# A decoder layer on one core: attention probabilities turned by VectorE blocks and SBUF transfers, value products in 128 rows, scores in eleven visits

## The chip, the core and the metric

One of the cores of one Trainium2 chip runs the whole layer. The metric is the device time of one execution in microseconds (us). A kernel's time is the median of its runs.

## The reference, cut to what matters

The layer takes x (512 positions x 1024) and mixes it in two ways. Mixer A is sparse attention with 8 heads of 64 in two groups of 4. Each query attends in three branches: to 31 compressed blocks, to selected blocks of 64 keys, and to a window of 512 keys. With 512 positions there are 8 blocks and up to 16 are selected, so the selected branch sees every earlier key, as the window does. The two therefore differ by their keys and values alone. Mixer B is a gated linear recurrence (HGRN2) with 4 heads.

```python
h = x @ w_in[l] + b_in[l]            # 5912 columns
ss = einsum('bghqd,bgqld->bghql', qr, ksel) * scale
ps = masked_softmax(ss, msel)        # the same for the window: sw, pw
o_slc = einsum('bghql,bgqld->bghqd', ps, vsel)
out_a = gt0 * o_cmp + gt1 * o_slc + gt2 * o_win
y = sigmoid(gm_a) * ((out_a * silu(z_a)) @ w_branch_a) + sigmoid(gm_b) * (o_b @ w_branch_b)
x = layer_norm(alpha * x + y @ w_out, ln_g, ln_b)
```

All is float32.

## The kernel before, in words

A float32 product is made of three products of a rounded kind: each operand is split by `split2` into a rounded part (a ScalarE cast) and a rest (a VectorE subtraction), and hi x hi, hi x lo, lo x hi are summed in PSUM.

**Projections.** The input projection runs in tiles of 128 output columns by 512 positions, named in `M_TILES`: qb, the keys and values, q, the gates z, and the merge gates ga and gb in pairs. `proj` computes one: 8 pieces of the contraction by three products, 24 products of 512 columns. At its start it issues the load of the weights three tiles ahead and the split of those two tiles ahead; three buffers hold each of raw, hi and lo. `SEQ` is the order of the tiles after qb and i. The tile v is computed as four groups of products of 280 columns (`proj_v`). Then come the two branch projections in the order of `BRANCH`, and the output projection with the layer norm.

**The weave.** TensorE and SP (whose queue issues nearly all DMAs) execute in the order in which the program is written; VectorE and ScalarE are ordered by a scheduler at build time. The order on TensorE is set by hand: `_Weave.tick` is called four times in a tile (twice in each of the four groups of v, twice for each half tile of the branches), and each tick resumes those chains (Python generators) that are due. A chain writes some instructions and yields a number of ticks; these numbers are in the table `D`. So attention, the recurrence and the compression are laid between quarter tiles of projections.

**Attention.** Positions are handled in blocks of 128 queries, i = 3 down to 0, over 128 * (i + 1) keys. Six units (i, branches): the two branches apart for i = 3 and 2, together for 1 and 0. `attn_scores` starts after q3 and needs both keys, all four q tiles and the gates. A visit computes scores of one m (a pair of heads, ab = 0 and 1, in the lower and upper 64 rows of the array at once; three products each), two of them in the first unit: 22 visits. `masked` adds the mask and takes the row's extreme on VectorE, then ScalarE makes the exponential and its sum. When a unit is complete its probabilities are scaled by gate over sum, half by ScalarE, half by VectorE.

`attn_values` turns the probabilities on TensorE: for each step of 128 keys, sixteen transposes of 64 queries x 128 keys against an identity, into two PSUM banks, which `split2` evicts in two halves of 512 columns. Then four products of 512 columns add up `accs`. There are 8 + 6 + 4 + 2 = 20 steps. The compressed branch's values are put into `asum` first; `finish` adds each block's result to it. At the end `asum` is gated by silu(z_a) and split for the branch projection.

**Rows.** From ga1 to gb2 (`ROWS`, `LAST`) the projections run in halves of 64 rows (`proj_rows`), two tiles side by side, so that score visits there do not change the array's row form; `row_half` does the same for value products, with hand-overs through an empty GpSimd instruction.

**Buffers.** t2 has 63 buffers of 512 columns, t4 has 4 of 1024. The compression weights w1s lie in eight t2 buffers.

Of the kernel before, what the change touches and what calls it, by code (L numbers as in the profile page):

```python
# [18 lines left out]
P = 128  # L19
# [5 lines left out]
ROWS, LAST = "ga1", "gb2"  # L25

# [14 lines left out]
SEQ = "kcmp vcmp kslc kwin q0 q1 v zb0 q2 zb1 q3 zb2 zb3 za0 za1 za2 za3".split()  # L41
# [30 lines left out]
D = dict(h0=8, h2=4, h3=6, h4=2, h5=8, h6=4, n0=3, n1=2, n2=9, c0=1, c1=6, c2=7, c3=7,  # L72
         r0=5, p0=4, p1=9, p2=1, b0=2, a0=3, a1=0, a3=1, a4=1, a5=1, s0=15, s2=0, s3=1, a6=1, v0=2, v1=3, v2=2, v3=3, w0=2, w1=1, w2=2, w3=4, a7=2, a8=1)


class _Weave:


    def __init__(self):
        self.now, self.runs, self.late, self.edge = 0, [], [], 0  # L80
# [16 lines left out]

# [6 lines left out]
def layer_kernel(ctx: ExitStack, tc: tile.TileContext, xT, xn, w0, wi, wf, wv, small, brow, consts,  # L104
# [18 lines left out]
    t2 = ctx.enter_context(tc.tile_pool(name="t2", bufs=63))  # L123
    t4 = ctx.enter_context(tc.tile_pool(name="t4", bufs=4))
# [9 lines left out]
    def T4():  # L134
        return t4.tile([P, 2, 512], F32R, name="t4", tag="t4")
# [145 lines left out]

    LOWER, UPPER, FULL = slice(0, 64), slice(64, 128), slice(0, 128)
    narrow, half = [False], {}

    ORDER = mybir.DependencyInfo(mybir.DependencyClass.Sync, mybir.DependencyReason.DATA)

    def hand_over(*last):
        step = tc.keep_in_program_order(G.nop()).ins
        for m in last:
            tc.add_manual_dep(step, m.ins.name, ORDER, reason="last product in the rows before")  # L290
        return step

    def take(step, m):
        tc.add_manual_dep(m.ins, step.name, ORDER, reason="one bank, other rows of the array")

    def proj_any(name):
        return (proj, proj_rows)[M_INDEX[ROWS] <= M_INDEX[name] <= M_INDEX[LAST]](name)

    def product(ps, i, kt, x, r, start, stop):
        w, b = parts[i][x == 2], (xh, xl)[x == 1]  # L300
        return T.matmul(ps, w[r, 128 * kt:128 * kt + 128], b[kt][r], start=start, stop=stop)

    def products3(ps, i, kt):
        for x in range(3):
            product(ps, i, kt, x, FULL, kt == 0 and x == 0, kt == KT - 1 and x == 2)

    def proj_rows(name):
        i = M_INDEX[name]
        load(i + 3)
        split(i + 2)  # L310
        if i not in half:
            half[i] = PA()
            for kt in range(4):
                if kt % 2 == 0:
                    weave.tick()
                products3(half[i], i, kt)
            narrow[0] = True
        ps = half.pop(i)
        weave.edge = weave.now
        if i == M_INDEX[LAST]:  # L320
            narrow[0] = False
            for kt in range(4, KT):
                if kt % 2 == 0:
                    weave.tick()
                products3(ps, i, kt)
            return ps, 4 + i
        weave.tick()
        nxt = half[i + 1] = PA()
        for q in range(8):
            if q == 4:  # L330
                step = hand_over(one, two)
            if q in (2, 4, 6):
                weave.tick()
            lo, up = (LOWER, UPPER) if q < 4 else (UPPER, LOWER)
            for x in range(3):
                one = product(ps, i, 4 + q % 4, x, lo, False, q == 7 and x == 2)
                two = product(nxt, i + 1, q % 4, x, up, q == 0 and x == 0, False)
                if q == 4 and x == 0:
                    take(step, one)
                    take(step, two)  # L340
        return ps, 4 + i
# [225 lines left out]
    def cmp_kv():  # L567
        yield D["c1"]
        while None in mvs:
            yield 1  # L570
        hp = PS()
# [11 lines left out]
        yield D["c2"]  # L583
        ps = PT()
# [5 lines left out]
        yield D["c3"]  # L590
        ps = PT()
# [52 lines left out]
    def cmp_scores():  # L644

        while "cmp" not in ready:
            yield 1
        pg = PS(), PS()
# [11 lines left out]
    def cmp_probs(g, src):  # L660
        ps = transpose4(src)
# [17 lines left out]
        yield D["p1"]  # L679
        ps = transpose4(s)  # L680
# [5 lines left out]
    probs, pv_at = {}, [0]  # L686


    slot, alone = [-1, 0], [False]

    def visit(i):
        if weave.now != slot[0]:
            if narrow[0]:
                if (weave.now - weave.edge) % D["w%d" % i]:
                    return False
            elif weave.now < slot[1]:
                return False
        slot[:] = weave.now, weave.now + D["v%d" % i]
        return True
# [511 lines left out]
```

## Time and profile before

| | |
|---|---|
| time, median of 3 runs | 428.81 us (428.34 to 428.9) |
| span of the profiled execution | 427.3 us |
| what lies around the span, by the median of the runs | 1.5 us |
| TensorE busy | 420.1 us, 98% |
| VectorE busy | 290.2 us, 68% |
| ScalarE busy | 240.7 us, 56% |
| DMA moved | 47.6 MB, mean 111 GB/s |

The span runs from the first to the last instruction of one profiled execution; the page gives no other time of that execution. PE is TensorE's products, PEld its weight loads, DVE is VectorE, ACT ScalarE, POOL GpSimd, SP the queue that issues DMAs. A product's duration is its latency: products overlap, and what one costs is the distance between starts.

### The profile page before, as it was taken

How to read it: one execution, taken by the hardware profiler on the slowest of the kernel's cores; microseconds unless marked ns; L12 is line 12 of the kernel's file. 1: busy time of each engine (PE TensorE's matmuls, PEld its weight loads, DVE VectorE, ACT ScalarE, POOL GpSimd, SP SyncE). 2: the span in 40 equal slices, each digit the busy share in tenths (PEclk: the TensorE clock that was granted, in tenths of full speed). 3: DMA queues.
4: the chain of work that ended last, by engine and by line, in shares of the span. 5: the costliest groups of instructions: out<-in, count | busy, mean ns of one | idle time of the engine just before them, and what ended most of it. 6: DMA issues, size and time to landing. Idle time of an engine off the chain costs nothing.

```text
span 427.3 us, 6625 instructions
## 1 busy us (share of the span) xinstructions
PE 420.1 (98%) x2471; PEld 347.2 (81%) x2471; DVE 290.2 (68%) x592; ACT 240.7 (56%) x489; POOL 9.9 (2%) x22
## 2 busy tenths in 40 slices
PE   8999999999999999999999999999999999999994
PEld 7888888888898878876878978777788888888884
DVE  4925578995665569867665677368466977873683
ACT  3534533624346535588676777678687865538301
POOL 2000000000001220000000000000000000000000
PEclk9999999999999999999999999999999999999998
DMA  8995600243340555311311131111433640153031
GB/s 266 377 392 146 218 0 2 74 125 81 108 135 2 138 188 166 98 52 49 100 51 51 51 98 51 50 51 49 149 122 102 222 129 20 51 164 132 3 147 49
DMA packets 21024, 47.60 MB, mean 111 GB/s; under 512 B 2944, under 2 KB 4864, under 8 KB 20992
## 3 DMA queue, kind: packets, MB, share of 16 engines
q1 hardware_dynamic: 20560, 46.79, 33.5%
q8 instruction: 19, 0.31, 0.3%
q10 hardware_dynamic: 432, 0.39, 0.3%
q14 instruction: 13, 0.11, 0.1%
HBM read 41.93 MB, written 2.10 MB: 103 GB/s over the span
## 4 chain that ended last, share of the span: by engine, by line
PE 97%; DMA 1%; DVE 0%; SPq 0%; issue 0%; DVEq 0%; ACT 0%; ACTq 0%
PE pa L112 62%; PE pss L112 16%; PE pso L112 11%; PE pst L112 4%; PE pst L116 3%; DMA t<-in_w_dram 1%; SPq L119 0%; DVE t L1128 0%; PE pss L116 0%; DVE t L203 0%; DVE t L1125 0%; DVEq L1207 0%; ACT t L1123 0%; DVE sm_ss L1126 0%; ACTq L1123 0%
## 5 line engine op out<-in xcount | busy, mean ns | idle before, releaser
L112 PE MATMUL pa<-t,whi 128*128 128x512 f32 (+1 forms) x688 | 201.7, 394 | 0.0
L112 PEld LDWEIGHTS pa<-t,whi 128*128 128x128 f32 (+1 forms) x688 | 120.5, 188 | 26.9 <-issue 3.1
L112 PE MATMUL pa<-t,wlo 128*128 128x512 f32 (+1 forms) x344 | 127.1, 391 | 0.0
L160 DVE TENSOR_TENSOR wlo<-wraw,whi 128x1024 fp32r<-128x1024 f32 x46 | 56.5, 1232 | 43.9 <-ACT whi L159 42.7
L159 ACT CAST whi<-wraw 128x1024 fp32r<-128x1024 f32 x46 | 48.3, 1049 | 48.6 <-PE pa L112 33.8
L112 PEld LDWEIGHTS pa<-t,wlo 128*128 128x128 f32 (+1 forms) x344 | 61.9, 187 | 12.4
L736 ACT ACTIVATE t<-t,sm_mn 128x512 f32<-128x512 f32 (+3 forms) x64 | 35.6, 558 | 23.7 <-DVE sm_mn L733 20.5
L112 PE MATMUL pa<-t,t 128*128 128x512 f32 (+1 forms) x168 | 36.7, 375 | 0.0
L112 PEld LDWEIGHTS pa<-t,t 128*128 128x128 f32 x168 | 30.4, 188 | 5.6
L112 PE MATMUL pss<-t,t 128*128 128x512 f32 (+3 forms) x222 | 34.5, 311 | 0.0
L112 PE MATMUL pso<-t,t 128*128 128x512 f32 (+2 forms) x158 | 32.9, 344 | 0.6 <-DVE t L203 0.6
L160 DVE TENSOR_TENSOR t<-pst,t 128x512 fp32r<-128x512 f32 x38 | 24.5, 686 | 10.7 <-ACT t L159 10.7
L733 DVE CUSTOM_DVE_ANT_0 t<-pss,t 128x384 f32<-128x384 f32 (+3 forms) x60 | 25.9, 473 | 8.3 <-PE pss L112 8.2
L112 PEld LDWEIGHTS pss<-t,t 128*128 128x128 f32 (+1 forms) x222 | 27.3, 175 | 3.4 <-issue 0.7
L112 PEld LDWEIGHTS pso<-t,t 128*128 128x128 f32 x158 | 25.3, 190 | 4.6 <-ACT t L202 0.8
L160 DVE TENSOR_TENSOR t<-t,t 128x512 fp32r<-128x512 f32 (+1 forms) x26 | 17.4, 681 | 15.6 <-ACT t L159 15.5
L159 ACT CAST t<-t 128x512 fp32r<-128x512 f32 (+1 forms) x26 | 15.2, 604 | 20.1 <-DVE t L1044 14.8
L112 PE MATMUL pso<-t,vv 128*128 128x512 f32 (+1 forms) x96 | 24.5, 412 | 0.0
L159 ACT CAST t<-pst 128x512 fp32r<-128x512 f32 x38 | 20.1, 578 | 0.0
L112 PE MATMUL pss<-t,whi 128*128 128x512 f32 x64 | 19.7, 390 | 0.0
L116 PEld LDWEIGHTS pst<-con,t 64*128 64x128 f32 (+1 forms) x333 | 16.3, 138 | 3.0 <-issue 0.7
L112 PE MATMUL pss<-kh,t 64*128 64x512 f32 (+2 forms) x88 | 18.1, 389 | 0.1
(188 smaller groups left out, 510.7 us busy)
## 6 DMA issues: line engine op xcount, KB each, us to landing
wraw<-in_wf_dram SPq DMA_DIRECT2D x38, 512.0 KB, 3.8
wraw<-in_wbr_dram SPq DMA_DIRECT2D x8, 512.0 KB, 3.9
t<-in_wout_dram SPq DMA_DIRECT2D x16, 256.0 KB, 3.2
t<-in_w_dram SPq DMA_DIRECT2D x15, 256.0 KB, 6.3
t<-t SPq DMA_DIRECT2D x48, 64.0 KB, 2.0
t<-in_wi_dram SPq DMA_DIRECT2D x8, 256.0 KB, 6.0
t<-in_xn_dram SPq DMA_DIRECT2D x8, 256.0 KB, 5.8
t<-in_xT_dram SPq DMA_DIRECT2D x7, 256.0 KB, 5.2
```

The costliest lines, as they stand in the source:

```text
L112: return tc.keep_in_program_order(nc.tensor.matmul(*a, **k))
L116: return tc.keep_in_program_order(nc.tensor.transpose(*a, **k))
L159: A.copy(dst_hi, src)
L160: V.tensor_tensor(dst_lo, src, dst_hi.bitcast(F32), ALU.subtract)
L733: V.tensor_tensor_reduce(out=p[:, c], in0=dsts[m, ab][:, c], in1=amask[:, 512 - n:512], op0=ALU.add, op1=ALU.min, scale=-0.125, scalar=3.0e38,
L736: A.activation(p[:, c], p[:, c], AF.Exp, bias=mn[:, h:h + 1], scale=-1.0, accum_out=den[:, h:h + 1])
```

## The change

Attention's probabilities are no longer turned by TensorE. VectorE transposes them in blocks of 32 x 32 into a buffer `blocks`, and sixteen DMAs for each unit, SBUF to SBUF and issued by SP, put the blocks of 32 rows in their places in a second buffer (`TURN`). The result is split from there, in one piece of 1024 columns for each step, the rest being written in place. The value products use all 128 rows, and the projections too: `proj_rows`, `row_half` and the hand-overs are gone. A score visit takes two m (four in the last unit), so there are 11. Each pair of m is scaled by itself (`soften`). Keys and queries come ahead of the compression tiles in `SEQ`, and `attn_scores` starts when v begins. `claim` keeps chains that share PSUM banks apart by ticks. `attn_sum` adds the compressed values to those blocks that are already finished and copies them to the others. The last b branch comes ahead of the a branches. The compression weights, then `blocks`, then the residual rows x share one buffer of 4096 columns (`BIG`); i's rounded weights, then the turned probabilities, share another (`TURN`). The delays in `D` are new.

```diff
-SEQ = "kcmp vcmp kslc kwin q0 q1 v zb0 q2 zb1 q3 zb2 zb3 za0 za1 za2 za3".split()
+SEQ = "kslc q0 kwin q1 v q2 q3 kcmp vcmp zb0 zb1 zb2 zb3 za0 za1 za2 za3".split()
-BRANCH = [("b", 0), ("b", 2), ("b", 4), ("a", 0), ("a", 2), ("b", 6), ("a", 4), ("a", 6)]
+BRANCH = [("b", 0), ("b", 2), ("b", 4), ("b", 6), ("a", 0), ("a", 2), ("a", 4), ("a", 6)]
+D = dict(h0=6, h2=4, h3=7, h4=0, h5=5, h6=3, n0=6, n1=7, n2=4, c0=1, c1=5, c2=5, c3=4, r0=5, p0=5, p1=5, p2=2, s0=8,
+         s2=5, s3=0, v0=10, v1=8, v2=7, v3=8, e0=4, e1=3, t0=6, t1=5, t2=4, t3=5, t4=1, a5=0)
+    def claim(self, ticks):
+        while self.now < self.held:
+            yield 1
+        self.held = self.now + ticks
-    t2 = ctx.enter_context(tc.tile_pool(name="t2", bufs=63))
-    t4 = ctx.enter_context(tc.tile_pool(name="t4", bufs=4))
+    t2 = ctx.enter_context(tc.tile_pool(name="t2", bufs=57))
+    t4 = ctx.enter_context(tc.tile_pool(name="t4", bufs=3))
+    big = ctx.enter_context(tc.tile_pool(name="big", bufs=1))
+    turn = ctx.enter_context(tc.tile_pool(name="turn", bufs=1))
...
     def attn_scores():
-        while not {"keys0", "keys1", "gates"} <= ready or len(QAB) < 4:
-            yield 1
+        blocks.append(BIG())
         for u, (i, brs) in enumerate(units):
...
+            for ms in ((0, 1, 2, 3),) if i == 0 else ((0, 1), (2, 3)):
+                while not {"keys%d" % b for b in brs} <= ready or not set(ms) <= set(QAB):
                     yield 1
+                yield from weave.claim(D["e0"])
...
                 weave.late.append(masked)
+                weave.start(soften(u, ms, ts, den), D["e1"])
+                yield D["v%d" % i]
+
+    def soften(u, ms, ts, den):
...
+        yield D["t0"]
+        while turned[0] < u:
+            yield 1
+        nst = nb * (i + 1)
+        view = blocks[0][:, 0:1024 * nst].rearrange("p (b c h s) -> p c b h s", b=4, h=8, s=32)
+        for ab in range(2):
+            for m in ms:
+                V.transpose(view[:, :, :, 4 * ab + m],
+                            ts[m, ab][:, 0:128 * nst].rearrange("p (c b s) -> p c b s", b=4, s=32))
+        if ms[-1] == 3:
+            yield D["t3"]
+            while spent[0] < u:
+                yield 1
+            w = TURN()
+            to = w.bitcast(F32)[:, 0:1024 * nst].rearrange("p (a x) -> p a x", a=4)
+            of = blocks[0][:, 0:1024 * nst].rearrange("p (b x) -> p b x", b=4)
+            for a in range(4):
+                for b in range(4):
+                    dma(to[32 * b:32 * b + 32, a], of[32 * a:32 * a + 32, b])
+            turned[0] = u + 1
+            yield D["t1"]
+            for st in range(nst):
+                part = w[:, 0:1024 * nst].rearrange("p (a c x) -> p c a x", a=4, x=256)[:, st]
+                weave.start(values(u, st, part), D["t4"] * st)
+
+    def values(u, st, lo):
+        i, brs = units[u]
+        br, j = brs[st // (i + 1)], st % (i + 1)
+        hi = T4().rearrange("p (a x) -> p a x", a=4)
+        split2(lo.bitcast(F32), hi, lo)
+        yield D["t2"]
...
+        for ab in range(2):
+            for k, t in enumerate((hi, lo)):
+                T.matmul(accs[i][ab], vts[j][:, br, 128 * ab:128 * ab + 128],
+                         t[:, :, 128 * ab:128 * ab + 128],
+                         start=(br, j) == (0, 0) and k == 0, stop=(br, j) == (1, i) and k == 1)
+        if st == (i + 1) * len(brs) - 1:
+            spent[0] += 1
...
+    wish = TURN()
...
-    w1s = [[T2() for _ in range(4)] for _ in range(2)]
+    w1b = BIG()
...
-                weave.start(attn_scores(), D["s0"])
-                weave.start(attn_values())
+                weave.start(attn_sum())
...
         if name == "v":
+            weave.start(attn_scores(), D["s0"])
             proj_v()
...
-            ps, m = proj_any(name)
+            ps, m = proj(name)
...
-    res = [[T2(), T2()] for _ in range(4)]
+    resb = BIG()
...
-    nc = _bacc.Bacc("TRN2", target_bir_lowering=False, num_devices=1)
+    nc = _bacc.Bacc("TRN2", target_bir_lowering=False, num_devices=1, dynamic_dma_scratch_size=1024)
```

## Rows read from the trace of the kernel before

**Rows 1.** The page: busy us, share of the span and instructions of the engines, the granted clock of TensorE in 40 slices of the span (tenths of full speed), and the engines' shares of the chain that ended last.

```profile
PE 420.1 (98%) x2471; PEld 347.2 (81%) x2471; DVE 290.2 (68%) x592; ACT 240.7 (56%) x489; POOL 9.9 (2%) x22
...
PEclk9999999999999999999999999999999999999998
...
PE 97%; DMA 1%; DVE 0%; SPq 0%; issue 0%; DVEq 0%; ACT 0%; ACTq 0%
```

**Rows 2.** Timeline of ScalarE where a tile is evicted (start us, us, engine, line, operation), za0 and gb7, and from the chain of waits one whole tile (start us, us, what, number of products).

```profile
177.72 0.68 ACT L962 ACTIVATE t<-pa,sml 128x512 f32<-128x512 f32 x1
...
335.52 0.68 ACT L1016 ACTIVATE t<-pa,hbias 128x512 f32<-128x512 f32 x1
...
84.30 5.47 PE pa L112 x24
```

**Rows 3.** The chain of waits, 262 to 271 us: start us, us, what. pst is the transposes' bank, pso the values', pss the scores', pa the projections'.

```profile
262.20 0.49 PE pst L116 x16
262.69 1.13 PE pso L112 x4
263.83 2.73 PE pa L112 x12
266.56 0.93 PE pso L112 x4
```

**Rows 4.** The chain of waits again: a group of four transposes of the compressed probabilities, the first of the compressed values and the tile that follows them.

```profile
183.64 0.44 PE pst L116 x4
...
197.10 0.57 PE pso L112 x2
...
198.15 2.07 PE pa L112 x8
```

**Rows 5.** Timeline of TensorE around one score visit.

```profile
269.85 0.39 PE L112 MATMUL pa<-t,wlo 128*128 128x512 f32 x1
270.17 0.50 PE L112 MATMUL pss<-kh,t 64*128 64x512 f32 x2
270.50 0.40 PE L112 MATMUL pss<-kl,t 64*128 64x512 f32 x2
270.74 0.40 PE L112 MATMUL pss<-kh,t 64*128 64x512 f32 x2
271.07 0.73 PE L112 MATMUL pa<-t,whi 128*128 128x512 f32 x2
271.64 0.39 PE L112 MATMUL pa<-t,wlo 128*128 128x512 f32 x1
```

**Rows 6.** VectorE's groups by line and shape, 118 to 336 us (busy us, mean ns | idle before them and what ended it), and from the whole span the reordering addition.

```profile
L160 DVE TENSOR_TENSOR wlo<-wraw,whi 128x1024 fp32r<-128x1024 f32 x29 | 35.9, 1237 | 36.9 <-ACT whi L159 35.8 <-PE pso L112 0.9
L160 DVE TENSOR_TENSOR t<-pst,t 128x512 fp32r<-128x512 f32 x38 | 24.5, 686 | 10.7 <-ACT t L159 10.7
L733 DVE CUSTOM_DVE_ANT_0 t<-pss,t 128x384 f32<-128x384 f32 x16 | 8.3, 553 | 1.3 <-PE pss L112 1.2
...
L733 DVE CUSTOM_DVE_ANT_0 t<-pss,t 128x256 f32<-128x256 f32 x16 | 6.0, 419 | 1.1 <-PE pss L112 1.1
...
L753 DVE TENSOR_SCALAR t<-t,sm_dn 128x512 f32<-128x512 f32 x8 | 3.4, 481 | 0.1
...
L753 DVE TENSOR_SCALAR t<-t,sm_dn 128x384 f32<-128x384 f32 x8 | 2.9, 416 | 0.1
...
L753 DVE TENSOR_SCALAR t<-t,sm_dn 128x256 f32<-128x256 f32 x8 | 2.4, 350 | 0.1
...
L560 DVE TENSOR_TENSOR t<-t,sml 128x496 f32<-128x496 f32 x4 | 4.2, 1087 | 0.0
```

**Rows 7.** The stretch 118 to 336 us: its length, busy us (and instructions) of each engine, granted clock, DMA share, GB/s.

```profile
118.00:336.00 218.00, 217.94 (x1458) 176.81 (x1457) 146.86 (x324) 146.71 (x313) 7.22 (x8) 1.00 0.29 91
```

**Rows 8.** ScalarE's groups by line and shape, 118 to 336 us.

```profile
L159 ACT CAST whi<-wraw 128x1024 fp32r<-128x1024 f32 x29 | 30.5, 1051 | 30.2 <-PE pa L112 23.2 <-issue 7.0
L159 ACT CAST t<-pst 128x512 fp32r<-128x512 f32 x38 | 20.1, 578 | 0.0
```

**Rows 9.** Timeline of SP's queue, 139 to 148.3 us (start us, us of issue, what, number), and the list of DMA issues (KB each, median us from issue to landing).

```profile
139.51 2.41 SPq L119 DMA_DIRECT2D t<-t  x4
142.02 0.53 SPq L119 DMA_DIRECT2D wraw<-in_wf_dram  x1
142.64 4.95 SPq L119 DMA_DIRECT2D t<-t  x8
...
t<-t SPq DMA_DIRECT2D x48, 64.0 KB, 2.0
```

**Rows 10.** Timeline of SP's queue: the 27th and 28th loads of weights. Timeline of ScalarE: the 27th cast of weights. List of issues: the landing.

```profile
194.95 7.96 SPq L119 DMA_DIRECT2D wraw<-in_wf_dram  x2
...
214.68 1.05 ACT L159 CAST whi<-wraw 128x1024 fp32r<-128x1024 f32 x1 [2.33 <-issue]
...
wraw<-in_wf_dram SPq DMA_DIRECT2D x38, 512.0 KB, 3.8
```

**Rows 11.** The chain of waits: the products with the compression weights.

```profile
94.42 1.90 PE pss L112 x32
...
97.91 1.90 PE pss L112 x32
```

More of the change, by code (lines that the diff above doesn't have):

```diff
@@ L23 @@
 EPS = 1e-5
-ROWS, LAST = "ga1", "gb2"
 AHEAD = 1
@@ L134, in T4, with BIG, TURN @@
     def T4():
-        return t4.tile([P, 2, 512], F32R, name="t4", tag="t4")
+        return t4.tile([P, 1024], F32R, name="t4", tag="t4")
+    def BIG():
+        return big.tile([P, 4096], F32, name="big", tag="big")
+    def TURN():
+        return turn.tile([P, 4096], F32R, name="turn", tag="turn")
     def SM(n, name):
@@ L277, in proj @@
             T.matmul(ps, lo[:, c], xh[kt], start=False, stop=kt == KT - 1)
-        return ps, 4 + i
[L282 to L340, printed above, removed]
         return ps, 4 + i
@@ L570, in cmp_kv @@
             yield 1
+        yield from weave.claim(5)
         hp = PS()
@@ L583, in cmp_kv @@
         yield D["c2"]
+        yield from weave.claim(2)
         ps = PT()
@@ L590, in cmp_kv @@
         yield D["c3"]
+        yield from weave.claim(2)
         ps = PT()
@@ L644, in cmp_scores @@
     def cmp_scores():
-        while "cmp" not in ready:
+        while "cmp" not in ready or len(qraw) < 4:
             yield 1
+        yield from weave.claim(2)
         pg = PS(), PS()
@@ L660, in cmp_probs @@
     def cmp_probs(g, src):
+        yield from weave.claim(2)
         ps = transpose4(src)
@@ L679, in cmp_probs @@
         yield D["p1"]
+        yield from weave.claim(2)
         ps = transpose4(s)
@@ L758, in attn_values, with attn_sum @@
+    def attn_sum():
         while len(PTc) < 2:
             yield 1
-        for _ in range(6):
-            if weave.now != slot[0] or not alone[0]:
-                yield 1
-        pc = [PO(), PO(), PT(), PT()]
+        yield from weave.claim(3)
+        pc = [PS(), PS(), PT(), PT()]
         for g in range(2):
@@ L795, in row_half @@
-        def row_half(it, q, step=None):
-            begin, end = (bank(it)[0], False) if step is None else (False, it[1:3] == (1, it[0]))
-            for k in range(2):
-                ms = []
-                for ab in range(2):
-                    ms.append(T.matmul(*operands(it, ab, k, UPPER if q ^ ab else LOWER), start=begin and k == 0,
-                                       stop=end and k == 1))
-                    if step and k == 0:
-                        take(step, ms[-1])
-            return ms
@@ L873, in attn_values @@
-        while owed or prev:
+            c = 512 - 128 * finished[0]
+            if c:
+                (A.copy, V.tensor_copy)[m % 2](asum[:, m, 0:c], pc[m][:, 0:c])
+            if c < 512:
+                V.tensor_tensor(asum[:, m, c:512], asum[:, m, c:512], pc[m][:, c:512], ALU.add)
+        ready.add("sum")
+        while finished[0] < 4:
             yield 1
-            second() if owed else whole(prev.pop(0))
         yield D["a5"]
@@ L902, in layer_kernel @@
     w2s = T2(192)
-    w1s = [[T2() for _ in range(4)] for _ in range(2)]
+    w1b = BIG()
+    w1s = [[w1b[:, 2048 * a + 512 * j:2048 * a + 512 * j + 512] for j in range(4)] for a in range(2)]
     dma(w2s, w2)
```

166 lines of the change are left out of this document (46 added, 120 removed).

## The prediction

> **What bounds the kernel now.** I read the busy shares and the chain of waits first. TensorE is busy 98% of the span, the chain that ended last is TensorE for 97%, and the granted clock is at its upper level, 2.4 GHz, in every slice but the last [rows 1]. So time is won only where TensorE loses instructions, or the edges between them, and lost where it must wait for an operand. Next I looked for a stretch that holds only whole projection tiles and attention: from the eviction of za0 at 177.72 to that of gb7 at 335.52, 157.8 us [rows 2]. It holds 19 tiles of 24 products; one undisturbed tile is 5.47 us, 0.228 per product of 512 columns [rows 2]. 19 x 5.47 = 103.9, so 53.9 us are attention's.
>
> These 53.9 split so. The values: 20 steps (8 + 6 + 4 + 2) of four products, 0.93 each [rows 3], 18.6. The scores: pairs of 64-row products that run side by side; 36 pairs of 512 columns, 24 of 384, 12 of 256 make 60 pairs of 512, at 0.228: 13.7. Two groups of four compression transposes at 0.44, and the compressed values, 197.10 to 198.15 [rows 4]: 1.9. That leaves 19.7. The sixteen 64x64 transposes of a step stand in the chain with 0.49 us [rows 3]: 20 x 0.49 = 9.8. The other 9.9 must be edges. The view of single products shows one: from the last full product at 269.85 to the third after the visit at 271.64 is 1.79 us for one product, three pairs and two products, 6 x 0.228 = 1.37 [rows 5]. So one visit to 64-row work costs 0.42 at its two edges, and 9.9 us are some 23 of them, which agrees with 22 score visits and 20 transposing ones, partly shared, partly inside the stretch where the projections themselves run in 64 rows.
>
> **The change, part by part.**
> *Transposes off TensorE:* -9.8 us, all on the path.
> *Fewer edges:* scores in 11 visits of twelve products (24 in the last), value products in 128 rows, which need no visit. 11 x 0.42 = 4.6 instead of 9.9: -5.3. The hand-overs of the row halves lie in that number.
> *Value products, scores, projections:* the same columns, 0.
> *Order of tiles and branches:* every tile still runs once; 0 on TensorE. It gives attention room: counted in weave ticks (a quarter tile) from the start of v, score visits stand at 8, 16, 24, 32, 40, 47, 54, 61, 68, 76 and 84, transfers at 30, 46, 61, 75, 90 and 104, the last value product at 115. Attention's branch begins at 136, so the end has some 17 ticks of cover, 17 x 1.37 = 23 us and more.
> *Buffers and sums:* six 512-column buffers and one of the value buffers fewer, against two of 4096 columns; the compressed values may now be added after the first units instead of before, in the same additions. 0: a buffer that comes free late delays VectorE or ScalarE, which have the ticks of the next points. The smaller scratch of the DMA rings touches none of the queues in the trace.
> *VectorE:* 48 block transposes, 24 of 512 columns, 16 of 384, 8 of 256. The trace shows no such instruction. Cheapest neighbours: the scalings, 481, 416 and 350 ns [rows 6], together 21.0 us. Dearest: the addition that reorders its operand, 1087 ns for 496 elements [rows 6], 2.19 ns per element, over 20480 columns 44.9. I take the plain one-pass rate (686, 553 and 419 ns, [rows 6]), 28.7, since both a copy's reading and a strided write lie within one pass. The splits go from 40 of 512 columns (686 from PSUM) to 20 of 1024 (1237): 27.4 to 24.7, -2.7. From 118 to 336 us VectorE was busy 146.9 of 218 [rows 7]; afterwards 172.9 of some 203, 85%. That is hidden if nothing is due within an instruction or two; the schedule leaves five or six ticks a stage (7 to 8 us). ScalarE loses 40 x 578 and gains 20 x 1051 ns [rows 8]: -2.1, nothing on the path.
> *Transfers:* six groups of sixteen. Four SBUF transfers of 64 KB took 2.41 us of SP's queue, eight took 4.95 [rows 9], so 0.60 to 0.62 each, whatever their bytes I take 0.61. A group is 9.8 us of issue, and lands 2.0 later [rows 9]. Then one cast 1.05 and one subtraction 1.24: the first value product can start 14.1 us after the group's first issue. The schedule puts it 5 + 1 + 4 = 10 ticks later: 13.7 us of projections plus one score visit (six pairs, 1.37, and its edges 0.42), 15.5. Cover 1.4 us; cost taken 0. If landing doubles with the bytes to 4.0, 0.6 a unit is exposed, 3.6 in all.
> *What queues behind them on SP:* the weight loads, in program order. Load 27 was issued at 194.95 and its cast began at 214.68 [rows 10]: 19.7 us ahead, of which landing takes 3.8. A block of 9.8 leaves 6. Nothing on the path; if SP also had to wait over 6 us inside a group, the cast would be late, and only after another tile TensorE.
> *A new wait:* the blocks share one buffer with the compression weights (BIG, a single one). The 64 products that read these, in two runs of 1.90 us [rows 11], now come after vcmp, at ticks 29 and 30, while the first unit's transposes are written at 17 and 25. They must wait: eight transposes (5.5), then 14.1: 19.6 us after those products, against 10 ticks with one visit less their last run, about 15. So the first unit can be 4.6 late. If the transposes run into the gap, or the tick count is off by two or three, it is 0. I take 2.2; both ends stay in the range. Behind it wait SP's next loads (covered as above).
>
> Sum, against the profiled span: 427.3 - 9.8 - 5.3 + 2.2 = 414.4. The median of the runs, 428.81, is 1.5 above that span; I add it: **415.9, say 416**.
>
> **The rivals.**
> *A, as above,* 413.5 to 420: its own doubts are the first unit (0 to 4.6) and 0.6 a unit at landing; with neither it is 412.2 + 1.5 = 413.7.
> *B, VectorE becomes the bound.* For: it is already 67% busy in this stretch and idles for others: 36.9 us before the weight subtractions and 10.7 before the splits, nearly all for ScalarE [rows 6]. Suppose half of this, 24, cannot be filled. With 28.7 of transposes the sum is 172.9 + 24 = 197, under 203: no bound. With 44.9 it is 213, 10 us over: 426. Against: the schedule is deep, and dear forms in this trace are those with reordered reads, while here the write is strided. The Trainium skill ("VectorE: DVE Perf Modes", section "The three transpose paths") gives 311 ns for a 128x128 bf16 block by VectorE against 390 by TensorE, and a 4x4 grid of 32x32 turns for it; an estimate from that page, 160 such blocks, is 50 us, and by it the sum would be 218, 15 over, which eats the whole gain. No run here shows this instruction yet.
> *C, slower: the transfer group through SP is the bound.* Place: the first value product of each unit, TensorE waiting for the cast of the landed block. If an issue costs 1.0 us for 128 KB instead of 0.61 for 64 KB, the group takes 16 + 2.0 + 2.3 = 20.3, 4.8 over the cover of 15.5, six times: 29 us, 443 in the end. It decides at 2.5 us a unit over the cover (428.8 - 1.5 - 412.2 = 15.1, over 6), that is from 0.86 us an issue on. For: one buffer takes the turned data, so nothing can be sent ahead. Against: SP's issue of a weight load of 512 KB took 0.53 in the same minute as 64 KB took 0.61 [rows 9], so bytes don't set it.
> *D, more than that goes:* no wait at all, and a few of the edges around compression and recurrence too, up to six of them: 411 to 413.5.
> *E, nothing comes of it:* B's and C's half sizes together, about 428.8.
>
> **How the numbers follow.** A 0.62, D 0.06, B 0.15, C 0.12, E 0.05. Predicted 416. The range leaves out C, the upper end of B and the lowest of D: 411.5 to 427. Faster by over 0.2% (0.9 us, about what a measurement here can tell): A, D and most of B, 0.83; within it 0.04; slower 0.13.
>
> **What would show it.** The chain should hold no 64-row transposes and eleven visits of 64-row scores; the same 19 tiles with attention, though begun earlier, should cost about 15 us less over the whole. VectorE's new instruction should read near 0.69 us for 512 columns and VectorE 85% from 118 us on; a group of sixteen should occupy SP for under 10 us. A gap on TensorE ahead of the first value products of the first unit alone, of 0 to 5 us, is my doubt; a gap ahead of every unit is C; late evictions of scores or tiles, with TensorE waiting for VectorE, are B. The prediction is wrong if TensorE idles over 8 us between 118 us and the branches, or if the value products cost more than 0.93 a step.

## The result and the profile after

The changed kernel takes 426.62 us (median of 4 runs, 425.65 to 427.06) where the kernel before took 428.64 beside it: ratio 0.9947, 95% interval 0.9932 to 0.9962. It is faster, by 2.0 us; 12.8 were forecast. The profiled execution's span is 425.2 us, against 427.3.

The page of the changed kernel: busy us, share and instructions of the engines, the granted clock in 40 slices, shares of the chain that ended last.

```profile
PE 409.8 (96%) x2063; PEld 334.2 (79%) x2063; DVE 314.8 (74%) x636; ACT 239.2 (56%) x469; POOL 10.1 (2%) x22
...
PEclk9999999999999999989999999999999999999999
...
PE 78%; DVE 8%; ACT 5%; SPq 4%; DMA 2%; issue 2%; DVEq 0%; ACTq 0%
```

Against [rows 1], TensorE lost 408 instructions and 10.3 us of busy time, but the chain now leaves it for a fifth of the span: it waits for VectorE, ScalarE and SP's queue. From 30 us to its last product TensorE is idle for 0.06 us before and 8.9 after. To see where that lies, and what else moved, I cut both spans at the first product behind i's tiles, at the first branch's second run of products and at the first product of the output projection. Timeline of TensorE, the kernel before, then the changed one:

```profile
70.77 0.62 PE L112 MATMUL pa<-t,whi 128*128 128x512 f32 x2
...
336.79 0.62 PE L112 MATMUL pss<-t,whi 128*128 128x512 f32 x2
...
377.59 11.04 PE L112 MATMUL pst<-t,t 128*128 128x512 f32 x48
```

```profile
69.86 0.62 PE L115 MATMUL pa<-t,whi 128*128 128x512 f32 x2
...
326.03 0.62 PE L115 MATMUL pss<-t,whi 128*128 128x512 f32 x2
...
374.27 9.68 PE L115 MATMUL pst<-t,t 128*128 128x512 f32 x42
384.62 1.92 PE L115 MATMUL pst<-t,t 128*128 128x512 f32 x6 [0.68 <-ACT t L170]
```

In us against the kernel before; a wait is counted from start to start, with the refilling behind it:

| from the first product behind i's tiles to the first branch's second run of products | |
|---|---|
| work that left TensorE (transposes, edges), by difference from the sum | -14.0 |
| the last unit's eight value products, now inside the branches | -1.9 |
| waits: 1.1 at the second visit (142.55), 3.3 at the first unit (184.3 to 187.9) | +4.4 |
| ten products behind that wait in 3.98 us (187.90 to 191.88), 0.425 each for most of them, instead of 0.228 each, 2.28 (the other 0.1 of the difference is refilling, counted with the wait) | +1.6 |
| sum (266.02 before, 256.17 after) | -9.9 |
| the last stretch: those eight value products 1.9; waits in the first a branch 5.5; waits ahead of and inside the first products of the output projection 1.2; 0.1 not assigned | +8.7 |
| the start, ahead of all this | -0.9 |

The 0.9 is luck of this execution and not the change: in the profiled executions of the thirteen variants of the changed kernel below, the first mark lies at 70.1 to 71.1, in the three of the kernel before at 70.6 to 70.8.

VectorE's groups by line and shape, after: busy us, mean ns, idle before. It is the instruction that no row of before showed.

```profile
L710 DVE STREAM_TRANSPOSE big<-t 128x512 f32<-128x512 f32 x24 | 15.3, 681 | 1.0 <-PE pss L115 1.0
L710 DVE STREAM_TRANSPOSE big<-t 128x384 f32<-128x384 f32 x16 | 7.8, 544 | 0.0
L710 DVE STREAM_TRANSPOSE big<-t 128x256 f32<-128x256 f32 x8 | 2.7, 407 | 0.0
```

Four stretches of the changed kernel: length, then busy us (instructions) of TensorE, its weight loads, VectorE, ScalarE, GpSimd; granted clock; DMA share; GB/s.

```profile
118.00:326.00 208.00, 204.16 (x1028) 159.97 (x1028) 164.26 (x353) 136.84 (x280) 6.91 (x9) 0.99 0.47 133
184.20:188.00 3.80, 0.97 (x6) 0.52 (x5) 3.62 (x7) 3.25 (x5) 0.00 (x0) 1.00 0.00 0
188.00:191.00 3.00, 3.00 (x8) 2.31 (x9) 3.00 (x4) 2.37 (x3) 0.00 (x0) 0.56 0.00 0
191.00:195.00 4.00, 4.00 (x20) 2.94 (x18) 4.00 (x6) 0.15 (x1) 0.00 (x0) 0.90 0.38 130
```

In the first, which answers to [rows 7], VectorE is 79% busy. In the second TensorE works 0.97 of 3.80 us; in the third, right behind it, it is never idle, but at a granted clock of 0.56, near the lower of its levels (1.2 GHz): the eight products from 188.23 to 191.50 take the time of fourteen.

**The first unit.** SP's queue, then ScalarE, after: start us, us, what, and in brackets the idle time before and what ended it.

```profile
164.30 10.05 SPq L122 DMA_DIRECT2D turn<-big  x16
...
318.04 10.01 SPq L122 DMA_DIRECT2D turn<-big  x16
328.09 1.08 SPq L122 DMA_DIRECT2D t<-in_wout_dram  x2
329.27 0.38 SPq L122 DMA_DIRECT2D wraw<-in_wbr_dram  x1
```

```profile
178.80 0.73 ACT L679 ACTIVATE t<-t,sm_mn 128x512 f32<-128x512 f32 x1 [2.13 <-DVE sm_mn L676]
...
185.23 0.27 ACT L551 COPY vcB<-pst 128x128 f32<-128x128 f32 x1 [0.51 <-DVE kcB L550]
185.54 2.94 ACT L170 CAST t<-turn 128x1024 fp32r<-128x1024 f32 x3
```

The group of sixteen was issued from 164.30 to 174.35, and its last piece landed at 176.2. Its cast stands at 185.54, 9.3 us later. ScalarE was not busy all that time: it stood 2.13 us for exponentials of a later visit and 0.51 for a copy of the compressed values. Both stand ahead of the cast in ScalarE's order, which was fixed when the program was built. TensorE, after:

```profile
186.64 0.51 PE L115 MATMUL pso<-t,vv 128*128 128x512 f32 x1 [2.07 <-ACT t L170]
187.90 0.50 PE L115 MATMUL pso<-turn,vv 128*128 128x512 f32 x1 [0.75 <-DVE turn L171]
...
188.94 0.63 PE L115 MATMUL pso<-t,vv 128*128 128x512 f32 x1
189.37 0.63 PE L115 MATMUL pso<-turn,vv 128*128 128x512 f32 x1
```

**The tail.** ScalarE and TensorE, after, 329 to 355 us.

```profile
329.52 2.00 ACT L170 CAST t<-turn 128x1024 fp32r<-128x1024 f32 x2 [3.37 <-DMA turn<-big]
...
335.67 1.05 ACT L170 CAST whi<-wraw 128x1024 fp32r<-128x1024 f32 x1 [2.25 <-DMA wraw<-in_wbr_dram]
...
338.59 1.19 ACT L747 COPY t<-pso 64x512 f32<-64x512 f32 x2
...
345.93 0.62 ACT L170 CAST t<-asum 128x512 fp32r<-128x512 f32 x1 [2.61 <-DVE asum L781]
```

```profile
348.50 0.70 PE L115 MATMUL pa<-t,whi 128*128 128x512 f32 x2 [1.38 <-DVE t L942]
...
350.88 0.50 PE L115 MATMUL pa<-t,whi 128*128 128x512 f32 x1 [1.21 <-DVE t L171]
...
352.08 0.50 PE L115 MATMUL pa<-t,whi 128*128 128x512 f32 x1 [0.24 <-DVE t L171]
...
354.60 0.50 PE L115 MATMUL pa<-t,whi 128*128 128x512 f32 x1 [1.56 <-DVE t L171]
```

The last group can be issued only at 318.04, when the unit before has left the one buffer; it holds SP until 328.05. Behind it the weights of a branch go out at 329.27. So ScalarE stands twice, 3.37 us for the group and 2.25 for those weights, and the copy of the last accumulator, in order behind them, starts at 338.59, though its products had ended at 334.9. The sums and their casts follow, and the first a branch, which reads them, waits four times, 4.4 us idle in all. From 336.75 to 355 VectorE is busy for 18.12 of 18.25 us: between the sums stand splits of branch weights and of output weights, so its order has a share in these waits that no run separates.

### The profile page after: what moved, and what is told of

It reads as the page before. It is cut to its first block, busy times and chain, and to the rows that moved or that the text cites. A ratio compares the mean times of both kernels' runs of the same rounds, so it can differ in the third digit from the quotient of the medians.

```text
span 425.2 us, 5979 instructions
## 1 busy us (share of the span) xinstructions
PE 409.8 (96%) x2063; PEld 334.2 (79%) x2063; DVE 314.8 (74%) x636; ACT 239.2 (56%) x469; POOL 10.1 (2%) x22
## 4 chain that ended last, share of the span: by engine, by line
PE 78%; DVE 8%; ACT 5%; SPq 4%; DMA 2%; issue 2%; DVEq 0%; ACTq 0%
PE pa L115 51%; PE pso L115 12%; PE pss L115 12%; SPq L122 4%; PE pst L115 2%; DMA wraw<-in_wbr_dram 1%; DVE t L171 1%; DVE big L710 1%; ACT t L170 1%; DVE t L942 1%; DVE wlo L171 1%; ACT whi L170 1%; PE pst L119 1%; ACT t L679 1%; DVE t L899 1%
## 5 line engine op out<-in xcount | busy, mean ns | idle before, releaser
L115 PE MATMUL pa<-t,whi 128*128 128x512 f32 x640 | 201.5, 395 | 4.4 <-DVE t L171 3.0
L115 PEld LDWEIGHTS pa<-t,whi 128*128 128x128 f32 x640 | 118.6, 189 | 34.6 <-DVE t L171 4.3
L115 PE MATMUL pa<-t,wlo 128*128 128x512 f32 x320 | 125.0, 391 | 0.0
L115 PEld LDWEIGHTS pa<-t,wlo 128*128 128x128 f32 x320 | 60.2, 188 | 12.8
L115 PE MATMUL pss<-t,t 128*128 128x512 f32 (+2 forms) x158 | 30.6, 324 | 0.0
L171 DVE TENSOR_TENSOR turn<-turn,t 128x1024 fp32r<-128x1024 f32 x20 | 23.6, 1215 | 7.3 <-ACT t L170 7.2
L710 DVE STREAM_TRANSPOSE big<-t 128x512 f32<-128x512 f32 (+2 forms) x48 | 25.8, 590 | 1.0 <-PE pss L115 1.0
L115 PEld LDWEIGHTS pss<-t,t 128*128 128x128 f32 x158 | 24.0, 190 | 2.9
L170 ACT CAST t<-turn 128x1024 fp32r<-128x1024 f32 x20 | 20.0, 1048 | 3.8 <-DMA turn<-big 3.4
L170 ACT CAST t<-t 128x512 fp32r<-128x512 f32 (+1 forms) x18 | 10.6, 595 | 17.5 <-DVE t L946 12.7
L115 PE MATMUL pa<-turn,t 128*128 128x512 f32 x64 | 19.9, 389 | 0.0
```

The costliest lines, as they stand in the source:

```text
L115: return tc.keep_in_program_order(nc.tensor.matmul(*a, **k))
L170: A.copy(dst_hi, src)
L171: V.tensor_tensor(dst_lo, src, dst_hi.bitcast(F32), ALU.subtract)
L710: V.transpose(view[:, :, :, 4 * ab + m], ts[m, ab][:, 0:128 * nst].rearrange("p (c b s) -> p c b s", b=4, s=32))
```

## The experiments

Fifteen runs in five batches; a letter in a quoted expectation names a theory of its own batch. Times are medians; the ratio is to the kernel before, run on the same chip (428.7 to 429.1 us).

### First batch: when, how many transfers, which buffer, how much VectorE

**e1**, score visits closer together, so that every unit comes sooner:

```diff
-         s2=5, s3=0, v0=10, v1=8, v2=7, v3=8, e0=4, e1=3, t0=6, t1=5, t2=4, t3=5, t4=1, a5=0)
+         s2=5, s3=0, v0=10, v1=6, v2=6, v3=6, e0=4, e1=3, t0=6, t1=5, t2=4, t3=5, t4=1, a5=0)
```

> The changed kernel with shorter delays between score visits (D: v1, v2, v3 from 8, 7, 8 to 6), so that the last unit's transfers are issued at tick 149 instead of 165 and attention's sum is ready 16 ticks earlier. In the changed kernel TensorE loses 5.0 us in the first a branch, waiting for that sum. Theory T (attention simply ends too few ticks before its branch): the 5.0 us go, some 421.5 us. Theory S (SP: the last group of sixteen transfers holds back the loads of the branch weights, ScalarE stands behind the late cast, and the sum behind ScalarE): they go too, since the group now lies among gate tiles; 421.5. Theory V (VectorE has too much to do in this stretch): little, 425 to 427, with new waits for VectorE in the middle, where the units now follow each other faster.

446.87 us, ratio 1.0425 (1.0403 to 1.0448): a clear miss. The tail's waits went, but at each of the first five units TensorE now stood idle, for 4.0, 3.7, 3.6, 5.9 and 1.0 us. Two stretches of this run:

```profile
291.00:296.70 5.70, 0.50 (x1) 0.19 (x1) 5.70 (x10) 3.28 (x4) 0.00 (x0) 0.73 0.01 4
296.70:300.00 3.30, 3.23 (x8) 2.56 (x9) 3.30 (x4) 0.00 (x0) 0.00 (x0) 0.50 0.00 0
```

VectorE is busy through the whole wait: the subtraction that the product needs stands behind other work in its order, 4.85 us of the next unit's block transposes last. And the clock is at 0.50 afterwards. The units can't simply be moved forward.

**e2**, one transfer of all 128 rows for each unit instead of sixteen:

```diff
-            for a in range(4):
-                for b in range(4):
-                    dma(to[32 * b:32 * b + 32, a], of[32 * a:32 * a + 32, b])
+            dma(w.bitcast(F32)[:, 0:1024 * nst], blocks[0][:, 0:1024 * nst])
```

> The changed kernel with one transfer of all 128 rows for a unit in place of sixteen of 32 rows: the same bytes, one issue; the blocks are not put in their places, so the values are sums over wrongly placed probabilities. Ticks and order are the same. S: SP is free, the weights of the branches come in time, the 5.0 us in the first a branch go; the first unit's wait (3.3 us) shrinks to 0 or 1; about 419. T: the tail stays, only the first unit gains, about 423.5. V: both stay, 426.

This kernel leaves out the placing of the blocks. 420.03, ratio 0.979 (0.9778 to 0.9803). Issue 0.52 us instead of 10.05, the landing of 2 MB takes 9.1 from issue, and the cast follows it: landed 173.2, cast 173.86. The first unit's waits are gone, and of the tail's four one of 0.32 us is left (two of 0.43 and 1.31 come in at other places); so they hang on the sixteen issues and what these do to the order of the rest.

**e3**, the compression weights out of the shared buffer:

```diff
-    w1b = BIG()
+    w1b = TURN()[:].bitcast(F32)
```

with their loads moved behind i's tiles, which use that buffer first.

> The changed kernel with the compression weights in the buffer of the turned probabilities (TURN, loaded after i's tiles) instead of in that of the blocks (BIG): the first unit's transposes no longer wait for the products with these weights. If that shared buffer is what makes TensorE wait 3.3 us (in starts) ahead of the first unit's values, they go: about 423.3, and the tail's 5.0 stay. If the wait is that of the group of transfers alone (9.8 us of issue against ten ticks), at least 2 us of it stay: 425.5 to 426.6.

427.6 (9 runs), ratio 0.9965 (0.9952 to 0.9978): no gain. The transposes are done at 153.3, the group goes out 4.5 us sooner and lands at 172.4. ScalarE in that run:

```profile
186.66 0.27 ACT L551 COPY vcB<-pst 128x128 f32<-128x128 f32 x1 [0.51 <-DVE kcB L550]
186.97 2.94 ACT L170 CAST t<-turn 128x1024 fp32r<-128x1024 f32 x3
```

Blocks that landed 4 us sooner are cast 1.4 us later, behind the same copy (1.0 of the 1.4 is a later start of this execution). The shared buffer is not the cause.

**e4**, every block transpose done twice (`for _ in range(2): V.transpose(...)`), 25.8 us more of VectorE:

> The changed kernel with every block transpose on VectorE made twice: 48 more instructions of 590 ns, 25.8 us more for VectorE by the trace of the changed kernel. V: VectorE is near its limit, so much of it shows, 8 us or more, with TensorE waiting for VectorE from 118 us on. T and S: it is hidden but at the two places where TensorE waits already, the first unit (eight transposes in its chain, up to 4.7 us) and the tail: 1 to 6 us, 427.5 to 432.5.

447.49, ratio 1.0437 (1.0419 to 1.0455), 20.9 us slower, where V had said 8 or more. From 118 to 346 us VectorE is 82% busy (187.4 of 228), and yet the 25.8 us cost 20.9. TensorE's waits are at the value products, for casts and subtractions (0.5 to 3.6 us each at the first, second, fourth and fifth unit), and as before in the tail. I read this as a matter of what stands ahead of the instruction that a product needs, and not of the share.

### Second batch: other queues, other times

**e5**, every second transfer issued by GpSimd's queue:

```diff
+    def dma_pool(o, i):
+        tc.keep_in_program_order(G.dma_start(o, i))
...
-                    dma(to[32 * b:32 * b + 32, a], of[32 * a:32 * a + 32, b])
+                    (dma, dma_pool)[b % 2](to[32 * b:32 * b + 32, a], of[32 * a:32 * a + 32, b])
```

> The changed kernel with every second of a group's sixteen transfers issued by GpSimd's queue, which is idle; everything else as it was. Theory S (SP's ten microseconds of issue for a group hold back what follows: the branch weights at the tail, the group's own landing): SP's part falls to 5 us, the tail's two waits of ScalarE (3.4 us for the turned block, 2.2 for the weights) go, and with them most of TensorE's 5.0 us; 420 to 423. Rival Q (the order of ScalarE's and VectorE's instructions, fixed at build time, is what makes the values late, not the landing): the first unit's 3.3 us stay unless the order changes with it; 421.5 to 423. If GpSimd's issue is slower than SP's by more than double, the group lands no earlier and it is 426 or more.

**417.69** (417.48 to 417.81), ratio 0.9739 (0.9726 to 0.9751): 8.9 us below the changed kernel, the fastest of all. GpSimd's queue at the first and the last unit, then ScalarE at the first:

```profile
164.18 4.04 POOL L167 DMA_DIRECT2D turn<-big  x8 [5.58 <-DVE big L713]
...
313.71 3.93 POOL L167 DMA_DIRECT2D turn<-big  x8 [21.31 <-PE pso L115]
```

```profile
176.16 2.00 ACT L173 CAST t<-turn 128x1024 fp32r<-128x1024 f32 x2
...
191.07 0.24 ACT L554 COPY vcB<-pst 128x128 f32<-128x128 f32 x1
```

At the last unit the group is on the queues for 5.3 us instead of 10.0, and of the tail's four waits one of 0.44 is left. At the first unit SP's eight alone take 9.34 us and the group lands at 175.5, hardly sooner than 176.2; but the cast follows at once, and the copy that stood ahead of it stands 15 us behind it.

**e6**, the same with ScalarE's queue (`(dma, dma_act)[b % 2]`):

> The same with ScalarE's queue for every second transfer. SP's part is 5 us again, but ScalarE, 56% busy and in a fixed order, has to issue eight for a unit (some 0.4 to 0.6 each, 4 us) and to stand there until the blocks are turned. S alone: 421 to 423. Q: ScalarE's delays show at each unit and in late evictions, 425 to 435.

430.48 (428.63 to 433.76), ratio 1.0045 (1.0013 to 1.0078). Its issues stand in ScalarE's own order and wait there; at the first unit ScalarE stands 4.92 us. Two queues are no gain in themselves.

**e7**, the first unit's products three ticks later (`yield D["t2"] + 3 * (u == 0)`):

> The changed kernel with the first unit's value products three ticks later (t2 + 3 for unit 0 alone); the next unit's transfers come at tick 104, after the 99 at which these products then end, so nothing else moves. Q and S agree that its block has landed at 176 and is cast at 185.5, and TensorE asks at 184.3: with three ticks more the 3.3 us go, 423.3, and the tail stays. If the products of the first unit hold up something else (the accumulator banks, the buffer of turned blocks), less: 424 to 426.6.

434.38, ratio 1.0127 (1.0112 to 1.0141): a miss by 11 us. The wait did not go, it moved and grew: the second unit lands at 216.8, is cast at 230.4, and TensorE waits 5.21 and 1.40 us at 231.

**e8**, e5 and e1 together:

> Half the transfers on GpSimd and the shorter delays between visits of e1 (v1, v2, v3 = 6). With SP alone these cost 18 us, TensorE waiting 2 to 7 us at each unit. S: the chain of a unit falls from 14.8 us (issue to values) to about 10, under the ten ticks, and the waits go: 418 to 422. Q: the casts stand behind ScalarE's work on later tiles and visits however early the block lands, and most of the waits stay: 435 to 445.

428.85, ratio 1.0003 (0.9988 to 1.0018), between the two expectations. The quicker group takes back 18 us of e1's 20, and TensorE still idles 8.6, by the trace for the banks of score visits, which come free late (5.2 of it), for two subtractions and at the second visit; none of these was changed by itself.

### Third batch: the two places apart, and the two terms of the saving

**e9**, GpSimd's half for the last unit alone (`[u == 5 and b % 2]`); **e10**, for the first five alone (`[u < 5 and b % 2]`).

> The changed kernel with half the transfers of the last unit alone on GpSimd's queue, the other five groups on SP as they were. ScalarE's order up to the first unit is that of the changed kernel. S at the tail: the last block lands some 9 us earlier against the first branch (320 instead of 329) and the branch weights behind it too; the 5.0 us of TensorE in the first a branch fall to under 1, and the first unit's 3.3 us stay: 421.5 to 422.5. If the tail's wait comes from the tick table (attention ending four ticks ahead of its branch) or from VectorE's load, 425 to 427.

> The mirror of it: half on GpSimd for the first five units, the last group on SP. Q: the first unit's block lands when it landed before (175 to 176), but its cast, in the new order of ScalarE, comes with it and not 9 us later; the first unit's 3.3 us go, and the wait for a score bank at 142 (1.1) with them; the tail keeps its 5.0: 421.5 to 423. If both places hang on the last group, 426.

e9: 423.36 (0.9866, 0.9847 to 0.9886); one wait of 0.44 is left at the tail, the first unit's 2.07 and 0.76 stay. e10: 422.17 (0.9842, 0.9827 to 0.9858); the first unit's cast stands at 176.25 and its wait is gone, the tail's 0.71, 1.20, 0.24 and 1.56 stay. The gains, 3.3 and 4.5 us, make 7.7 of e5's 8.9: two causes, nearly independent.

**e11**, the kernel *before* with each of TensorE's transposes done twice (`for _ in range(2): T.transpose(pq[h]...)`); **e12**, the kernel before with all projections in 128 rows (`return proj(name)`).

> The kernel before with each of attention's 320 transposes on TensorE made twice. It measures the first term of the forecast, 9.8 us for them. If TensorE alone sets the time and a transpose costs what its starts show (31 ns within a group, 0.49 for sixteen), +9.8: 438.5. If some of it lay beside other work, less, 432 to 436.

> The kernel before without the stretch of 64-row projections: every tile is computed in 128 rows, so score and transposing visits there have edges like all others. It measures the second term: the forecast took 0.42 us for an edge pair and 23 of them. Seven visits in that stretch become 7 x 0.42 = 2.9 us of edges, against the 2.3 us by which that stretch exceeds its products now, so 0 to +1 us: 428.7 to 429.8. If the hand-overs cost more than I think, it is faster than before, 426 to 428.

e11: 439.45, 1.024 (1.0225 to 1.0255): 10.35 us for 20 steps of sixteen transposes, 9.8 forecast. e12: 430.61, 1.0033 (1.0021 to 1.0044), 1.5 us, half a us over the upper end of what was expected: that is what the projections in 64-row halves had saved.

### Fourth and fifth batch: the order alone, no queue touched

**e13**, exponentials of later visits issued behind the cast that stands ahead of them in the program:

```diff
+                                with tc.issue_after(ahead[0]) if ahead[0] else nullcontext():
-                                A.activation(p[:, c], p[:, c], AF.Exp, bias=mn[:, h:h + 1], scale=-1.0,
-                                             accum_out=den[:, h:h + 1])
+                                    A.activation(p[:, c], p[:, c], AF.Exp, bias=mn[:, h:h + 1], scale=-1.0,
+                                                 accum_out=den[:, h:h + 1])
...
+        ahead[0] = cast.ins
```

> The changed kernel with one order altered and no queue: ScalarE's exponentials of later score visits are issued behind the last cast of a turned block that stands ahead of them in the program (before, they may be put ahead of it). Theory S (ScalarE's fixed order holds the landed block back): in the first unit the group still lands at about 176, but the cast stands at 179 to 183 instead of 185.5, TensorE's 3.3 us there shrink to under 1.5 and the eight products at 0.425 us go with them: 422.5 to 425. The tail's 5 us stay. Theory L (the landing or the transfers themselves hold it): cast at 185.5 as before, 426.6. A delay of exponentials could cost something at later score visits; over 428 would mean that the order around the cast matters more than the cast's own place.

426.99, ratio 0.9952 (0.994 to 0.9965): no gain, against S. ScalarE in that run:

```profile
185.63 0.27 ACT L551 COPY vcB<-pst 128x128 f32<-128x128 f32 x1 [2.54 <-DVE kcB L550]
185.94 1.99 ACT L733 CAST t<-turn 128x1024 fp32r<-128x1024 f32 x2
```

The exponentials are out of the way and the cast stands where it stood: behind the copy of the compressed values, for which ScalarE now stands 2.54 us with landed blocks to cast. That copy can't run sooner, since TensorE makes its operand at 184.3.

**e14**, the branches in the order of before:

> The changed kernel with the branches in the order of before (b6 behind two of the a branches). The first a branch then starts one b branch (48 products of 0.228, 10.9 us) sooner, while the sums that it reads come when they did (345 to 351). Theory T (the tail's waits are a matter of when the sums are ready against when the a branches start): 5.0 + 9 to 11 us of waits there, 434 to 438. If the order of branches only costs the 0.8 us ahead of the output projection: 425.8.

433.62, ratio 1.0113 (1.0097 to 1.0128), at T's lower edge. The cast of the sums stands where it stood (345.88, 345.93 after), the a branch wants them sooner: its waits are 6.9 us instead of 4.4, and from 346.5 to 358 the granted clock is 0.50. The waits at the output projection are gone. So the new order, with those waits, saves 7.0 us, and the last unit still comes too late for it.

**e15**, in the first unit the casts and subtractions go ahead of all that stood before them:

```diff
+    def behind():
+        es = ExitStack()
+        for ins in ahead:
+            es.enter_context(tc.issue_after(ins))
+        return es
...
+        if u == 0 and st < 2:
+            ahead.extend((cast.ins, sub.ins))
```

and `with behind():` around the exponentials, the tiles' first eviction and the copies to kcB and vcB.

> The changed kernel with every queue as it was. e13 moved the exponentials and left the cast where it was: behind the copy of the compressed values (L551), which waits for VectorE and TensorE until 185.6. Here the first unit's first two casts and subtractions are put ahead of what stood before them on ScalarE and VectorE: the exponentials, the next tile's eviction and the compression's copies are issued behind them. Theory S: the group lands at about 176 as before, the cast stands at 176 to 179.5 instead of 185.5, TensorE's 3.3 us at the first unit are gone and the eight products at 0.425 us with them; the tail's 5 us stay: 421 to 423, as in the kernel whose first five units use GpSimd's queue (422.2). Theory L (what the transfers or their queue do holds the cast): 426 to 427.

424.77 (423.08 to 425.72), ratio 0.9908 (0.9889 to 0.9927). The median lies 1.8 above what S gave at most, in runs that spread over 2.6 us; the profiled execution, the fastest of the five, took 423.08; its span is 421.3, 3.9 below that of the changed kernel's, which was the slowest of its four. ScalarE, then TensorE's two waits of over 0.2 us between 120 and 310 us, in that run:

```profile
177.85 1.99 ACT L743 CAST t<-turn 128x1024 fp32r<-128x1024 f32 x2
...
187.79 0.25 ACT L561 COPY vcB<-pst 128x128 f32<-128x128 f32 x1
```

```profile
187.81 0.50 PE L115 MATMUL pso<-turn,vv 128*128 128x512 f32 x1 [0.57 <-DVE turn L744]
...
223.73 0.50 PE L115 MATMUL pso<-turn,vv 128*128 128x512 f32 x1 [0.83 <-DVE turn L744]
```

SP issues as before (163.44, 10.05 us). Same queues, same landing, another order on two engines: the first unit's 3.3 us fall to 0.57, and from 184 to 195 us the clock stays at 1.00. That settles what made the first unit's cast late. It does not settle its whole price: by the medians the order gave 1.9 us back and not 4.9, a wait of 0.83 us is new at the second unit, and the spread of these runs is not explained. How much ScalarE's order did and how much VectorE's is not separated. The tail's waits (1.00, 1.20, 0.24, 1.55) stay.

## Why the prediction was right in part, and wrong by 10.6 us

It said 416.0; the time came out at 426.62. That this lies within the range is luck: rival A's own numbers end at 420, the range reached to 427 for part of rival B (426), and it was not B's mechanism that brought the time there.

*What held.* The transposes: 9.8 forecast, 10.35 by e11. Edges: 14.0 less 10.35 leaves some 3.6, where 5.3 stood; of a total of 15.1 forecast 14.0 came. VectorE's instruction: 681, 544 and 407 ns for 686, 553 and 419, so 28.3 us in durations for 28.7 (25.8 busy, since they overlap). The estimate of 50 us from the Trainium skill ("VectorE: DVE Perf Modes", "The three transpose paths") was too high for this form: by the row of 512 fp32 columns, 128 of them cost about 170 ns, where the page's 311 is for bf16, and the measurement decides. SP's group: 10.0 us for 9.8, its landing 2.4 for 2.0. At the last unit, cast and subtraction are done 13.8 us after the first issue (331.8), for 14.1. A gap ahead of the first unit's value products alone, of 0 to 5 us, was named as the doubt: 3.3 us came, for another reason than the one given.

*What failed, by its step.*

"Transfers: ... Cover 1.4 us; cost taken 0" and "hidden" for VectorE and ScalarE. These sums add durations as if each engine did next what is due next. At the first unit the chain took 22.3 us from issue to product, since the cast stood 9.3 us behind landed data. The prediction priced 2.2 us there, for the shared buffer ("A new wait"); that reason fell with e3. The price was 3.3 and, by the clock, 1.6 more, and e15 shows what made the cast late: the order on ScalarE and VectorE.

"What queues behind them on SP: ... Nothing on the path." I compared a projection's weight load, issued 19.7 us ahead [rows 10], with a group of 9.8. At the end of attention the margin isn't there: the branch weights left at 329.27 and ScalarE stood 2.25 us for them. e9, which shortens that one group, gives 3.3 us back; how much of that is the group's own landing and how much the weights behind it is not separated.

"Order of tiles and branches: ... some 17 ticks of cover." The built program has visits at ticks 8, 22, 34, 42, 50, 58, 66, 75, 82, 90 and 98, not 8 to 84; transfers at 36, 56, 72, 89, 104 and 117; the last value product at 127 and the sums at 129 to 132, with the a branch at 136. The cover is 4 ticks. My table left out that the second visit waits for the last query tiles, and the third for a claim that the compression holds. For the same reason the first unit's second pair is turned at tick 31 and not at 25, and its transfers stand at 36 and not at 30, which the working under "A new wait" had wrong too. The 13 ticks of cover that were not there are 17.8 us of tiles, more than three times the tail's 5.5.

Not in the prediction at all: the lower clock after a wait, 1.6 us, and the output projection's waits, 1.2.

In sum, in the span, from 414.4: +1.1 saved less, +2.2 waits, +1.6 clock, +5.5 first a branch, +1.2 output projection, +0.1 not assigned, -0.9 at the start, which makes 425.2. Rival C had the place right (the first value product waiting for the cast of the landed block) but its condition was an issue of over 0.86 us; it is 0.63 with its gap, and the group bounds only the tail. Rival B asked whether VectorE has time for its work; it does, at 79%, and yet e1 and e4 show waits behind it.

What stays open: what the first unit's order is worth over several executions (1.9 us by e15's median, 4.5 with e10's queue and order together); what VectorE's order in the tail costs, which no run changed by itself; and when a wait is followed by the lower clock (see the end). The order at the other units was not changed by itself either.

## What to carry to other kernels

Where an engine's order is fixed when the program is built, the cover of a transfer is not the sum of the durations behind it: look at what stands ahead of the consumer in its engine's order and when each of those gets its own operand, and if that is late, put the consumer first or change what makes it look late. A group of small DMAs through one queue delays whatever is behind it by the whole group, and the last group of a stage is where no margin is left; sharing that one with an idle engine's queue was worth 3.3 us here (e9). Sharing the others was worth 4.5 more (e10), but at the first unit by the order that the build then chose, not by an earlier landing. Delays counted in the source must be followed through every wait and claim before they are called cover.

## What the hardware showed that was not expected

Behind a wait TensorE's granted clock sometimes fell to its lower level: to 0.56 from 188 to 191 here, behind waits of 2.07 and 0.75 us; to 0.50 from 296.7 to 300 in e1, behind 1.08 and 4.77; to 0.50 from 346.5 to 358 in e14, where waits followed one another. At that level a product of 512 columns cost 0.425 us instead of 0.228, so the wait of 3.3 us here cost 4.9. The length of the wait alone did not decide it. In e3 the same products, behind waits of 1.92 and 0.76 us, ran at 1.00; and of the last of the tail's waits, 1.56 us in both kernels, the clock stayed at 1.00 behind the one here and fell to 0.53 behind the one in e4. The stretches of e3 and e4 behind these waits:

```profile
189.30:191.00 1.70, 1.68 (x6) 1.16 (x7) 1.70 (x3) 1.70 (x3) 0.00 (x0) 1.00 0.00 0
```

```profile
373.00:376.00 3.00, 2.89 (x7) 2.32 (x8) 3.00 (x6) 2.21 (x6) 0.00 (x0) 0.53 0.21 51
```

SP took 0.63 us for each 128 KB transfer between rows of SBUF, about what it took for 64 KB [rows 9]; GpSimd's queue took 0.50. A single transfer of 2 MB over 128 rows went out in 0.52 us and landed 9.1 after its issue, sooner than sixteen pieces from one queue (11.9).

The block transpose wrote 32-column pieces at a stride and cost no more than a plain pass [rows 6]: 681 ns against 686 for 512 columns.
